# Stick-breaking scores with a second pass over half the partitions, and the memory attention's scaling on GpSimd

## The chip, the core and the metric

The kernel runs on one core of a Trainium2 chip. The metric is device microseconds of that core for one execution of the whole program; lower is better. A core has a matrix engine (TensorE, PE in the rows; its weight loads are listed apart as PEld), a vector engine (VectorE, DVE), a scalar engine (ScalarE, ACT), GpSimd (POOL) and SyncE (SP), which issues most DMAs. Each works through its own queue in order; semaphores join them.

## The reference, cut to what matters

The model is a trunk of two layers over 512 positions and 1024 features. Layer 0 mixes with a gated delta net, layer 1 with stick-breaking attention; in both layers a quarter of the width goes through attention to 256 memory positions. The two pieces that the change touches:

```
z = einsum('bthd,bshd->bhts', q, k) * scale            # stick-breaking: 12 heads of 64 features
log_beta, log_1m_beta = log_sigmoid(z), log_sigmoid(-z) where s < t
tail = reverse cumsum(log_1m_beta) - log_1m_beta
a = exp(log_beta + tail) where s < t
o = einsum('bhts,bshd->bthd', a, v)

s = einsum('bshd,bmhd->bhsm', q, k) * scale             # memory attention: 4 heads of 64 features
p = softmax(s, axis=-1)
o = einsum('bhsm,bmhd->bshd', p, v)
```

## The kernel before

Products of fp32 matrices are made of three passes in a 32-bit format of TensorE that keeps fewer bits: every operand is split into a high part (hi) and the rest (lo), and hi·hi, hi·lo and lo·hi are summed. ScalarE makes the hi parts, VectorE subtracts them for the lo parts (`split_lo`, line 176, always `out = in - hi`).

The order in which instructions stand on each engine is set by a scheduler at build time from the order of the Python generators: `weave` mixes the delta net's recurrence with projections, and in layer 1 `stick_breaking` yields after every unit so that projections and memory attention are put between its units. No order is written out by hand around the change; what it does to the order is shown below.

**Stick-breaking (layer 1).** `sb_qk` projects q and k of one head as one piece: rows 0 to 63 of the result are q, rows 64 to 127 are k. From it three 128x512 tiles are made. `kk` holds k's lo part in rows 0 to 63 and k's hi part in rows 64 to 127. `qh` holds q's hi part in both halves. `ql` holds q's lo part in both halves, which takes two VectorE instructions of 64x512 (line 1075). There are 12 such pieces. `sb_scores` works on units: a unit is some of the four 128-key blocks of one head, and for each block it runs three matmuls into one PSUM bank: `kk` by `qh` over 128 rows (line 1092: lo·hi and hi·hi at once), the mask as a small bf16 matmul of 128 columns (line 1093), and `kk` by `ql` over 128 rows (line 1095: lo·lo and hi·lo). The last pass is the "second pass" of the title; there are 48. ScalarE then computes the logarithms (lines 1100 to 1102), VectorE the softplus `sb_e` (line 1103) and its parts `sp_h` and `sp_l` (lines 1107 and 176), TensorE the running sums (line 1122), ScalarE the exponential `sb_a` (line 1125), VectorE its hi part `sb_ah` (line 1128), GpSimd its lo part `sb_al` (line 1129), and TensorE the product with v (line 1141). A unit's scores, weights and values are issued two units apart.

**Memory attention (both layers).** `mem_attention` has eight units of one head and 256 queries. `scores` runs four matmuls (line 691), takes the maximum (line 694), the exponential with its sums (line 698) and the reciprocal of the sums (line 700, `sm`), and scales the 128x256 halves of `p` by it (line 702, two instructions a unit, 32 in all). `turn` transposes `p` on TensorE (line 711) and splits it into hi and lo; `values` multiplies by v (line 722). One unit's `turn` is issued behind the next unit's `scores`. Layer 0's units run beside the last group of the delta net (288 to 326 us in the profile), layer 1's beside the later stick-breaking units.

GpSimd's queue holds in both places also DMAs: the sums of weights for the MLP (line 882) and a gain (line 973), which waits until the last memory scores have read the buffer it writes.

Of the kernel before, what the change touches and what calls it, by code (L numbers as in the profile page):

```python
# [13 lines left out]
ALU = mybir.AluOpType  # L14
# [28 lines left out]
def f(ap):  # L43
    return ap.bitcast(F32)
# [23 lines left out]
class Trunk:  # L68
# [600 lines left out]
    def mem_attention(self, i, q, alloc, mixT):  # L669

        nc, v = self.nc, self.nc.vector
        kT, vv = self.mk[i], self.mv[i]
        if i == 1:
            wk, wv = alloc("w"), alloc("w")
            for w, d in ((wk, kT), (wv, vv)):
                nc.gpsimd.dma_start(out=w, in_=d[0])
            wk, wv = wk.rearrange("p (c m) -> p c m", c=2), wv.rearrange("p (t h d) -> p t h d", t=2, h=4)
            kT = [self.act.tile([P, 4, NMEM], F32R, name=f"mk0{x}") for x in "hl"]
            vv = self.act.tile([P, 2, 4, 2, 64], F32R, name="mv0")
            for c in range(2):  # L680
                self.both(kT, wk[:, c], c)
            nc.scalar.activation(out=vv[:, :, :, 0], in_=wv, func=AF.Copy)
            self.split_lo(vv[:, :, :, 1], wv, vv[:, :, :, 0])
        pT = {}

        def scores(h, t2):
            b = self.bank("acc").rearrange("p (t m) -> p t m", t=2)
            for j in range(2):
                ts = slice((t2 + j) * P, (t2 + j + 1) * P)
                for n in range(2):  # L690
                    nc.tensor.matmul(b[:, j], lhsT=q[h // 2][h % 2][:, ts], rhs=kT[n][:, h], start=n == 0,
                                     stop=n == 1)
            nm = self.small.tile([P, 2], F32, name="nmx")
            v.tensor_reduce(out=nm, in_=b, axis=AX.X, op=ALU.max, negate=True)
            sm = self.small.tile([P, 2], F32, name="sm")
            p = alloc("p")
            for j in range(2):
                nc.scalar.activation(out=p[:, j], in_=b[:, j], func=AF.Exp, bias=nm[:, j:j + 1],
                                     accum_out=sm[:, j:j + 1])
            v.reciprocal(out=sm, in_=sm)  # L700
            for j in range(2):
                v.tensor_scalar(out=p[:, j], in0=p[:, j], scalar1=sm[:, j:j + 1], scalar2=None, op0=ALU.mult)
            return p

        def turn(h, t2, p):
            if t2 == 0:
                pT[h] = alloc("pTh"), alloc("pTl")
            b = self.bank("acc").rearrange("p (m t) -> p m t", m=2)
            for m in range(2):
                for j in range(2):  # L710
                    nc.tensor.transpose(b[:, m, j * P:(j + 1) * P], p[:, j, m * P:(m + 1) * P], self.ident)
            sl = slice(t2 * P, (t2 + 2) * P)
            for m in range(2):
                nc.scalar.activation(out=pT[h][0][m][:, sl], in_=b[:, m], func=AF.Copy)
                self.split_lo(pT[h][1][m][:, sl], b[:, m], pT[h][0][m][:, sl])

        def values(h):
            p0 = 64 * (h % 2)
            pr, other = slice(p0, p0 + 64), slice(64 - p0, 128 - p0)
            b = self.bank("acc")  # L720
            for n, (k, r) in enumerate(((0, 0), (1, 0), (0, 1), (1, 1))):
                nc.tensor.matmul(b, lhsT=vv[:, k, h].rearrange("p a d -> p (a d)"), rhs=pT[h][r][k], start=n == 0,
                                 stop=n == 3)
            o = alloc("o")
            nc.scalar.activation(out=o[pr], in_=b[other], func=AF.Copy)
            v.tensor_tensor(out=mixT[pr, H + h // 2], in0=b[pr], in1=o[pr], op=ALU.add)

        units = [(h, t2) for h in range(4) for t2 in (0, 2)]
        prev = None
        for u in units + [None]:  # L730
            if u is not None:
                p = scores(*u)
                yield 4 * MM / 2
            if prev is not None:
                turn(*prev)
                yield 4 * MM / 2
                if prev[1] == 0 and prev[0] > 0:
                    values(prev[0] - 1)
                    yield 4 * MM
            prev = (*u, p) if u is not None else None  # L740
        values(3)
        yield 4 * MM
# [319 lines left out]
    def sb_qk(self, pair, hi, lo, pool, out):  # L1062

        nc, v = self.nc, self.nc.vector
        top, low = slice(0, 64), slice(64, P)
        for hh in range(2):
            qh, ql, kk = (pool.tile([P, S], F32R, name=f"sb{n}", bufs=4) for n in ("qh", "ql", "kk"))
            out[hh] = (qh, ql, kk)

            def done(b):  # L1070
                nc.scalar.activation(out=qh[top], in_=b[top], func=AF.Copy, scale=0.125)
                nc.scalar.activation(out=kk[low], in_=b[low], func=AF.Copy)
                nc.scalar.activation(out=qh[low], in_=b[top], func=AF.Copy, scale=0.125)
                for o in (top, low):
                    v.scalar_tensor_tensor(out=ql[o], in0=b[top], scalar=0.125, in1=f(qh[top]), op0=ALU.mult,
                                           op1=ALU.subtract)
                self.split_lo(kk[top], b[low], kk[low])
            yield from self.fm_slices(self.a["w_b_qk"][2 * pair + hh], hi, lo, done)

    def sb_scores(self, u, pool):  # L1080

        nc, v = self.nc, self.nc.vector
        qh, ql, kk = u["qk"][u["pr"].start // 64]
        u["zb"] = zb = self.bank("g")
        n = 0
        u["at"] = {}
        for i in u["blocks"]:
            t0 = i * P
            ks = slice(t0, t0 + P)
            u["at"][i] = slice(n, n + S - t0)  # L1090
            z = zb[:, u["at"][i]]
            nc.tensor.matmul(z, lhsT=kk[:, ks], rhs=qh[:, t0:], start=n == 0, stop=False, skip_group_check=True)
            nc.tensor.matmul(zb[:, n:n + P], lhsT=self.diag_bf, rhs=self.nmask, start=False, stop=False,
                             skip_group_check=True)
            nc.tensor.matmul(z, lhsT=kk[:, ks], rhs=ql[:, t0:], start=False, stop=True, skip_group_check=True)
            n += S - t0
        u["n"] = n
        z = zb[:, :n]
        e = pool.tile([P, S], F32, name="sb_e", bufs=4)[:, :n]
        nc.scalar.activation(out=e, in_=z, func=AF.Abs)  # L1100
        nc.scalar.activation(out=e, in_=e, func=AF.Exp, scale=-1.0)
        nc.scalar.activation(out=e, in_=e, func=AF.Ln, bias=1.0)
        v.scalar_tensor_tensor(out=e, in0=z, scalar=0.0, in1=e, op0=ALU.max, op1=ALU.add)  # L1103
        last = u["blocks"][-1]
        sh = pool.tile([P, n], F32R, name=f"sp_h{last}", bufs=2 if last else 1)
        sl = pool.tile([P, n], F32R, name=f"sp_l{last}", bufs=2 if last else 1)
        v.tensor_copy(out=sh, in_=e)
        self.split_lo(sl, e, sh)
        for i in u["blocks"]:
            u["head"]["sp"][i] = (sh[:, u["at"][i]], sl[:, u["at"][i]])  # L1110
# [258 lines left out]
```

## Time and profile before

| what | value |
| --- | --- |
| median of 3 runs | 1318.02 us (1313.18 to 1321.62) |
| the profiled execution | 1318.39 us |
| its span in the trace | 1316.7 us |
| mean granted TensorE clock | 0.993 of full speed |
| TensorE matmul busy | 1275.9 us (97%) |
| VectorE busy | 861.8 us (65%) |
| ScalarE busy | 717.5 us (54%) |
| GpSimd busy | 163.9 us (12%) |

The busy time of TensorE is modelled from its instructions and overlaps their tails, so 97% does not mean that the array streams all the time; where it streams without a gap, the starts of 512-column matmuls lie 0.23 us apart. The stick-breaking stage runs from about 760 to 926 us.

### The profile page before, as it was taken

Reading aid. Unit: us, or ns where it says so; the run is one execution under the profiler, and the core shown is the slowest. Engines: PE = TensorE matmul, PEld = TensorE weight load, DVE = VectorE, ACT = ScalarE, POOL = GpSimd, SP = SyncE. Lnnn points to the kernel's source line nnn. Section 1 sums busy time; section 2 is a strip of 40 time slices with the busy share of each in tenths; the row PEclk is TensorE's granted clock in tenths of the full one; section 3 lists DMA queues with packets and bytes.
Section 4 is the critical chain, followed back from the end, with each engine's and each line's share of the span. In section 5 each row is a group of like instructions: output and inputs, shape, how many; then the busy total and the mean of one; then the engine's idle time right before and its main releaser. Section 6 shows DMA issues by size and latency. Waiting matters only on the chain.

```text
span 1316.7 us, 18097 instructions
## 1 busy us (share of the span) xinstructions
PE 1275.9 (97%) x6620; PEld 1070.0 (81%) x6620; DVE 861.8 (65%) x1588; ACT 717.5 (54%) x1378; POOL 163.9 (12%) x196
## 2 busy tenths in 40 slices
PE   7999999998999999999999999998999999999997
PEld 7788878887788888878888988786788888878886
DVE  7677695877663264555788678999573255455776
ACT  8654435446455454444565567878455344454561
POOL 2511313010021000000000013223130000000000
PEclk9999999999999999999999999999999999999999
DMA  7551654415689878644454426222679944544441
GB/s 242 192 166 58 161 130 117 123 51 143 210 245 266 233 190 243 195 145 143 148 186 139 157 75 150 76 64 64 208 255 256 257 127 144 148 141 150 152 144 64
DMA packets 82153, 209.39 MB, mean 159 GB/s; under 512 B 6720, under 2 KB 11840, under 8 KB 81616
## 3 DMA queue, kind: packets, MB, share of 16 engines
q1 hardware_dynamic: 62192, 164.12, 37.7%
q0 software_dynamic: 19296, 43.06, 16.4%
q8 instruction: 52, 0.85, 0.3%
q10 hardware_dynamic: 576, 1.05, 0.2%
q14 instruction: 37, 0.30, 0.1%
HBM read 199.29 MB, written 67.63 MB: 203 GB/s over the span
## 4 chain that ended last, share of the span: by engine, by line
PE 80%; DVE 10%; ACT 6%; issue 2%; DMA 1%; POOL 0%; SPq 0%; DVEq 0%; POOLq 0%; ACTq 0%
PE ps_acc L212 45%; PE ps_g L955 21%; PE ps_g L212 4%; PE ps_g L526 1%; PE ps_g L1122 1%; DVE wlo L176 1%; PE ps_g L389 1%; PE ps_g L518 1%; ACT whi L199 1%; PE ps_g L488 1%; ACT scrap L281 1%; DVE cv L360 1%; PE ps_g L295 1%; DVE sb_e L1103 1%; PE ps_acc L1141 1%
## 5 line engine op out<-in xcount | busy, mean ns | idle before, releaser
L212 PE MATMUL ps_acc<-h_hi,whi 128*128 128x512 f32 (+1 forms) x888 | 338.1, 381 | 0.0
L212 PE MATMUL ps_acc<-h_hi,wlo 128*128 128x512 f32 (+1 forms) x888 | 337.5, 380 | 0.0
L212 PE MATMUL ps_acc<-h_lo,whi 128*128 128x512 f32 (+1 forms) x888 | 335.1, 377 | 0.0
L176 DVE TENSOR_TENSOR wlo<-raw,whi 128x1024 fp32r<-128x1024 f32 x134 | 169.2, 1264 | 141.3 <-ACT whi L199 133.9
L955 PE MATMUL ps_g<-whi,sh 128*128 128x512 f32 x784 | 261.1, 395 | 0.0
L199 ACT ACTIVATE whi<-raw 128x1024 fp32r<-128x1024 f32 x134 | 141.8, 1059 | 203.0 <-PE ps_g L955 94.1
L176 DVE TENSOR_TENSOR wlo<-xc,whi 128x1024 fp32r<-128x1024 f32 x89 | 108.8, 1224 | 151.2 <-ACT whi L199 149.0
L212 PEld LDWEIGHTS ps_acc<-h_hi,wlo 128*128 128x128 f32 x888 | 167.5, 189 | 34.0 <-DVE wlo L176 3.9
L212 PEld LDWEIGHTS ps_acc<-h_hi,whi 128*128 128x128 f32 x888 | 167.8, 189 | 28.8 <-ACT whi L199 1.6
L212 PEld LDWEIGHTS ps_acc<-h_lo,whi 128*128 128x128 f32 x888 | 167.9, 189 | 28.4
L955 PEld LDWEIGHTS ps_g<-whi,sh 128*128 128x128 f32 x784 | 147.6, 188 | 34.5
L199 ACT ACTIVATE whi<-xc 128x1024 fp32r<-128x1024 f32 x89 | 94.3, 1060 | 137.1 <-PE ps_g L955 92.5
L955 PE MATMUL ps_g<-wlo,sh 128*128 128x512 f32 x392 | 154.8, 395 | 0.0
L955 PEld LDWEIGHTS ps_g<-wlo,sh 128*128 128x128 f32 x392 | 73.9, 189 | 17.2
L882 POOL DMA_DIRECT2D sum<-w_down x56 | 51.5, 1332 | 181.8 <-DMA sum<-w_down 104.4
L176 DVE TENSOR_TENSOR sh<-ua,sh 128x512 fp32r<-128x512 f32 x98 | 66.7, 685 | 4.7 <-ACT sh L936 4.7
L1129 POOL TENSOR_TENSOR sb_al<-sb_a,sb_ah 128x384 fp32r<-128x384 f32 (+1 forms) x36 | 41.2, 1144 | 154.8 <-DVE sb_ah L1128 133.1
L936 ACT ACTIVATE sh<-ua 128x512 fp32r<-128x512 f32 x98 | 59.9, 618 | 0.3
L212 PE MATMUL ps_acc<-ua 128*128 128x512 f32 x224 | 57.3, 391 | 0.0
L978 POOL DMA_DIRECT2D ua<-park x4 | 2.3, 574 | 388.6 <-DVE sh L176 381.2
L212 PEld LDWEIGHTS ps_acc<-ua 128*128 128x128 f32 x224 | 42.0, 188 | 8.9
L212 PE MATMUL ps_acc<-whi,h_hi 128*128 128x256 f32 (+1 forms) x144 | 44.5, 326 | 0.0
(352 smaller groups left out, 2148.2 us busy)
## 6 DMA issues: line engine op xcount, KB each, us to landing
sum<-w_down POOLq DMA_DIRECT2D x56, 512.0 KB, 9.9
xc<-w_up SPq DMA_DIRECT2D x38, 512.0 KB, 3.9
xc<-w_down SPq DMA_DIRECT2D x30, 512.0 KB, 3.9
xc<-sum SPq DMA_DIRECT2D x29, 512.0 KB, 4.0
sum<-w_down SPq DMA_DIRECT2D x28, 512.0 KB, 6.5
sum<-sum SPq DMA_DIRECT2D x28, 512.0 KB, 5.4
raw<-w_in_a SPq DMA_DIRECT2D x27, 512.0 KB, 3.8
raw<-sum SPq DMA_DIRECT2D x27, 512.0 KB, 3.7
```

Of the source, the lines that this page charges most:

```text
L176: self.nc.vector.tensor_tensor(out=lo, in0=src, in1=f(hi), op=ALU.subtract)
L199: self.nc.scalar.activation(out=hi, in_=raw, func=AF.Copy)
L212: self.nc.tensor.matmul(out, lhsT=l, rhs=r, start=start and k == 0 and i == 0, stop=stop and k == n - 1 and i == 2)
L281: nc.scalar.activation(out=self.scrap(m), in_=x[:, j * m:(j + 1) * m], func=AF.Square, accum_out=ssq[:, j:j + 1])
L295: op = nc.tensor.transpose(b[:, j, i * P:(i + 1) * P], xs[i][:, (kc + j) * P:(kc + j + 1) * P], self.ident)
L360: nc.vector.scalar_tensor_tensor(out=acc[:, j:], in0=b[:, :S - j], scalar=w[:, 3 - j:4 - j], in1=acc[:, j:], op0=ALU.mult, op1=ALU.add)
L389: self.nc.tensor.transpose(tp[:, t], src(t), self.ident)
L488: nc.tensor.matmul(sb[:, j], lhsT=self.sel[:, s4 + j], rhs=ud, start=True, stop=True)
L882: self.tc.keep_in_program_order(nc.gpsimd.dma_start(out=dst, in_=src, accum_op=ALU.add))
L936: nc.scalar.activation(out=s[:, 0], in_=src, func=AF.Copy)
L955: nc.tensor.matmul(y[t], lhsT=l, rhs=r, start=new and d == 0 and z == 0 and m == 0, stop=d == nd - 1 and z == 1 and m == 2, skip_group_che ...
L1129: nc.gpsimd.tensor_tensor(out=u["al"], in0=a, in1=f(u["ah"]), op=ALU.subtract)
```

## The change

The `ql` tile is written in its lower half only (rows 64 to 127), and the second pass reads only those rows of `kk` and `ql`: it multiplies k's hi part with q's lo part and leaves the product of the two lo parts out. It streams as many columns as before, over 64 rows in place of 128. The scaling of `p` moves from VectorE to GpSimd.

```diff
@@ mem_attention, scores
             for j in range(2):
-                v.tensor_scalar(out=p[:, j], in0=p[:, j], scalar1=sm[:, j:j + 1], scalar2=None, op0=ALU.mult)
+                nc.gpsimd.tensor_scalar(out=p[:, j], in0=p[:, j], scalar1=sm[:, j:j + 1], scalar2=None, op0=ALU.mult)
@@ sb_qk, done
-                for o in (top, low):
-                    v.scalar_tensor_tensor(out=ql[o], in0=b[top], scalar=0.125, in1=f(qh[top]), op0=ALU.mult,
-                                           op1=ALU.subtract)
+                v.scalar_tensor_tensor(out=ql[low], in0=b[top], scalar=0.125, in1=f(qh[top]), op0=ALU.mult,
+                                       op1=ALU.subtract)
@@ sb_scores
-            nc.tensor.matmul(z, lhsT=kk[:, ks], rhs=ql[:, t0:], start=False, stop=True, skip_group_check=True)
+            nc.tensor.matmul(z, lhsT=kk[64:, ks], rhs=ql[64:, t0:], start=False, stop=True, skip_group_check=True)
```

Behind line 1075 every line number is one lower in the changed kernel.

How the order moves, first on GpSimd in layer 0's memory attention (`p` is the attention's probabilities, `Q` a tile of the delta net, `sum` the weight sums, `mk0h` the buffer of the gain):

```order
 L510 MEMSET Q 128x4x64 x2
+L702 TENSOR_SCALAR p<-p,sm 128x256 x10
 L882 DMA sum_0_4_603<-w_down 256x512
+L702 TENSOR_SCALAR p<-p,sm 128x256 x2
+L973 DMA mk0h<-norm_post_mlp 128x1024
+L702 TENSOR_SCALAR p<-p,sm 128x256 x4
 L882 DMA sum_1_4_607<-w_down 256x512
 L882 DMA sum_2_4_611<-w_down 256x512
 L882 DMA sum_3_4_615<-w_down 256x512
-L973 DMA mk0h<-norm_post_mlp 128x1024
 L586 TENSOR_TENSOR vb<-vb,fo 128x512
```

The sixteen scalings stand ahead of three of the four sums; the gain's DMA now stands ahead of the last four scalings, the seventh and eighth units'.

On GpSimd near the end of stick-breaking, the rows of before:

```order
L882 DMA sum_1_4_4719<-w_down 256x512
L1129 TENSOR_TENSOR sb_al<-sb_a,sb_ah 128x512
L1129 TENSOR_TENSOR sb_al<-sb_a,sb_ah 128x384 x2
L1129 TENSOR_TENSOR sb_al<-sb_a,sb_ah 128x512
L1129 TENSOR_TENSOR sb_al<-sb_a,sb_ah 128x384
L973 DMA mk0h<-norm_post_mlp 128x1024
```

and of the change:

```order
L882 DMA sum_1_4_4719<-w_down 256x512
L1128 TENSOR_TENSOR sb_al<-sb_a,sb_ah 128x512
L702 TENSOR_SCALAR p<-p,sm 128x256 x2
L1128 TENSOR_TENSOR sb_al<-sb_a,sb_ah 128x384
L702 TENSOR_SCALAR p<-p,sm 128x256 x2
L1128 TENSOR_TENSOR sb_al<-sb_a,sb_ah 128x384
L1128 TENSOR_TENSOR sb_al<-sb_a,sb_ah 128x512
L702 TENSOR_SCALAR p<-p,sm 128x256 x2
L973 DMA mk0h<-norm_post_mlp 128x1024
```

A pair of scalings now stands between the `sb_al` subtractions, one pair for one or two of them.

On VectorE, where the projections of stick-breaking's first pieces are taken apart:

```order
 L176 TENSOR_TENSOR wlo<-raw,whi 128x1024
-L1075 SCALAR_TENSOR_TENSOR sbql<-ps_acc,sbqh 64x512 x2
+L1074 SCALAR_TENSOR_TENSOR sbql<-ps_acc,sbqh 64x512
 L176 TENSOR_TENSOR sbkk<-ps_acc,sbkk 64x512
 L176 TENSOR_TENSOR wlo<-raw,whi 128x1024
-L1075 SCALAR_TENSOR_TENSOR sbql<-ps_acc,sbqh 64x512 x2
+L1074 SCALAR_TENSOR_TENSOR sbql<-ps_acc,sbqh 64x512
 L176 TENSOR_TENSOR sbkk<-ps_acc,sbkk 64x512
```

One instruction a piece is gone and its neighbours keep their places. In TensorE's queue the three matmuls of a block keep their places, too, except in the last units.

## Rows read from the trace of the kernel before

**Rows 1.** The page, part 1: busy time, share, instructions.

```profile
PE 1275.9 (97%) x6620; PEld 1070.0 (81%) x6620; DVE 861.8 (65%) x1588; ACT 717.5 (54%) x1378; POOL 163.9 (12%) x196
```

**Rows 2.** Windows of stick-breaking, early and late: busy us, PEclk, DMA share, GB/s.

```profile
755.00:835.00 80.00, 79.90 (x432) 67.23 (x431) 64.39 (x102) 57.10 (x104) 18.43 (x18) 1.00 0.47 122
835.00:926.00 91.00, 82.50 (x462) 66.50 (x461) 85.82 (x163) 72.59 (x160) 28.81 (x27) 1.00 0.22 57
```

**Rows 3.** The chain of waits by line, 755 to 835, then 835 to 926 us.

```profile
by line: PE ps_acc L212 63.3%; PE ps_g L1122 14.8%; PE ps_acc L1141 7.2%; PE ps_g L1095 5.7%; PE ps_g L1092 4.5%; PE ps_g L1093 2.1%; PE ps_acc L691 1.2%; DVE sp_h L1107 1.0%; DVE sb_e L1103 0.8%; DVE sb_ah L1128 0.4%; issue 0.0%
...
by line: issue 9.6%; DVE sb_e L1103 7.6%; DVE sp_l L176 7.5%; DVE sp_h L1107 7.5%; DVE p L702 4.5%; ACT sb_e L1101 3.8%; ACT p L698 3.7%; ACT whi L199 3.7%; POOL sb_al L1129 3.7%; ACT sb_e L1100 3.6%; PE ps_g L1122 3.6%; DVE sb_ah L1128 3.3
```

**Rows 4.** PE's timeline in one unit's scores: start, duration, line, tiles, shape.

```profile
783.18 0.22 PE L1092 MATMUL ps_g<-sbqh,sbkk 128*128 128x128 f32 x1
783.25 0.23 PE L1093 MATMUL ps_g<-nmask,diag_bf 128*128 128x128 bf16 x1
783.28 0.30 PE L1095 MATMUL ps_g<-sbql,sbkk 128*128 128x128 f32 x1
783.43 0.33 PE L1092 MATMUL ps_g<-sbqh,sbkk 128*128 128x256 f32 x1
```

**Rows 5.** Second passes: their weight loads, ns min/median/max; then groups early and late.

```profile
L1095 PEld LDWEIGHTS ps_g<-sbql,sbkk x48: 190/200/203, 762.7 to 910.2; 128*128 128x128 f32 x48
...
L1095 PE MATMUL ps_g<-sbql,sbkk 128*128 128x128 f32 (+3 forms) x23 | 8.9, 387 | 0.0
...
L1095 PE MATMUL ps_g<-sbql,sbkk 128*128 128x512 f32 (+3 forms) x25 | 9.8, 393 | 0.0
```

**Rows 6.** DVE groups, 835 to 926 us: busy us, mean ns, idle before.

```profile
L176 DVE TENSOR_TENSOR sp_l<-sb_e,sp_h 128x384 fp32r<-128x384 f32 x13 | 10.3, 795 | 0.2
...
L702 DVE TENSOR_SCALAR p<-p,sm 128x256 f32<-128x256 f32 x14 | 6.9, 532 | 0.1
L1075 DVE SCALAR_TENSOR_TENSOR sbql<-ps_acc,sbqh 64x512 fp32r<-64x512 f32 x10 | 6.8, 680 | 0.2
...
L1107 DVE CAST sp_h<-sb_e 128x384 fp32r<-128x384 f32 x13 | 6.0, 465 | 0.1
...
L1107 DVE CAST sp_h<-sb_e 128x512 fp32r<-128x512 f32 x8 | 4.7, 587 | 0.1
```

**Rows 7.** Line 702's durations over the whole run, ns min/median/max.

```profile
L702 DVE TENSOR_SCALAR p<-p,sm x32: 341/349/1409, 293.7 to 919.2; 128x256 f32<-128x256 f32 x32
```

**Rows 8.** DVE's timeline, undisturbed and beside GpSimd.

```profile
840.52 0.36 DVE L1107 CAST sp_h<-sb_e 128x384 fp32r<-128x384 f32 x1
840.91 0.56 DVE L176 TENSOR_TENSOR sp_l<-sb_e,sp_h 128x384 fp32r<-128x384 f32 x1
...
846.41 1.36 DVE L176 TENSOR_TENSOR sp_l<-sb_e,sp_h 128x384 fp32r<-128x384 f32 x1
...
848.88 0.42 DVE L1107 CAST sp_h<-sb_e 128x512 fp32r<-128x512 f32 x1
```

**Rows 9.** POOL's timeline: that subtraction, a later one, a memset, the gain's DMA.

```profile
846.06 1.29 POOL L1129 TENSOR_TENSOR sb_al<-sb_a,sb_ah 128x512 fp32r<-128x512 f32 x1 [5.71 <-DVE sb_ah L1128]
849.13 1.04 POOL L1129 TENSOR_TENSOR sb_al<-sb_a,sb_ah 128x384 fp32r<-128x384 f32 x1 [1.78 <-PE ps_acc L1141]
...
291.77 0.31 POOL L510 MEMSET Q<- 128x256 f32 x1 [8.03 <-PE ps_g L526]
...
310.86 0.61 POOL L973 DMA_DIRECT2D mk0h<-norm_post_mlp  x1 [13.32 <-PE ps_acc L691]
```

**Rows 10.** Waits of PE late in stick-breaking (total us, times, longest).

```profile
PE ps_acc L1141 <- POOL sb_al L1129: 1.7, 3, 0.8
```

**Rows 11.** Layer 0's memory attention: window, DVE group, PE's wait for it.

```profile
288.00:326.00 38.00, 32.58 (x207) 28.90 (x207) 28.02 (x80) 23.50 (x81) 4.80 (x7) 0.91 0.55 139
...
L702 DVE TENSOR_SCALAR p<-p,sm 128x256 f32<-128x256 f32 x16 | 4.9, 348 | 0.0
...
PE ps_acc L711 <- DVE p L702: 2.2, 3, 1.3
```

## The prediction, made before the changed kernel ran

> **What bounds the kernel now.** I read the page's busy shares first: TensorE is busy 97% of the span, VectorE 65%, GpSimd 12% [rows 1]. That is an average over stages, so I asked for the windows of the three places that the change touches. The reader is to see that the stick-breaking stage falls in two. From 755 to 835 us TensorE is busy 79.9 of 80 us, VectorE 64.4. From 835 to 926 us VectorE is busy 85.8 of 91 us, ScalarE 72.6, GpSimd 28.8, and TensorE's modelled 82.5 leaves at least 8.5 us free [rows 2]. The chain of waits says the same: early it is TensorE's lines almost alone, late it runs through VectorE's and ScalarE's short instructions, with line 702 itself at 4.5% of 91 us [rows 3]. So early every nanosecond added on TensorE counts and VectorE's relief is worth nothing; late it is the other way round. The granted clock is 1.00, the 2.4 GHz level, in both. In layer 0's memory attention (288 to 326 us) no engine is full: TensorE 32.6, VectorE 28.0 of 38 us [rows 11].
>
> **The second pass on TensorE.** Nothing is taken off it: 48 matmuls stay, of the same columns, 23 early and 25 late [rows 5]. What is new is that a matmul over rows 64 to 127 stands between two that use all 128 rows. The trace has no such change of rows, so its price p for one second pass must be bounded. Below: zero, since columns and weight loads stay; a gain only if a weight load of half the rows hid better, worth at most what is exposed today. That is read from the starts: `kk` by `qh` over 128 columns lets the next matmul start 0.07 us later, while the second pass over as many columns holds it for 0.15 us (783.28 to 783.43) [rows 4]: 0.08 us of a weight load that the short mask matmul before it cannot hide. Above: nothing of the neighbours overlaps any more. The mask matmul's record lasts 0.23 us where the next starts after 0.03, so 0.20; the second pass's lasts 0.30 where the next starts after 0.15, so 0.15 [rows 4]; a weight load of 0.20 us [rows 5] ahead of each change of rows, 0.40; less the 0.08 exposed already: 0.67 us. I take p = 0.09 us, one more weight load exposed as one is today, since that is the nearest row: also a neighbour that cannot be overlapped in full, and it costs that much. Early that is 23 x 0.09 = **+2.1 us** (bounds 23 x -0.08 = -1.8 and 23 x 0.67 = +15.4). Late 25 x 0.09 = 2.3 us fits into TensorE's 8.5 us.
>
> **VectorE late in stick-breaking.** Two things leave its queue between 835 and 926 us: half of ten line 1075 instructions, 5 x 0.680 = 3.4 us, and 14 scalings, 6.9 us [rows 6]. GpSimd takes them. An operation of this kind by GpSimd is in no row. The nearest below is a memset of 128x256, 0.31 us, which reads nothing; above, the subtraction of 128x384 with two inputs, 1.04 us [rows 9]. I take 0.7 us, the subtraction's time by columns (256 of 384), because a scaling reads and writes as it does. Fourteen are 9.8 us, and GpSimd then has 28.8 + 9.8 = 38.6 of 91 us: not a bound.
>
> But GpSimd's work slows VectorE. While `sb_al` ran from 846.06 to 847.35, `sp_l` of 128x384, begun at 846.41, took 1.36 us in place of 0.56 [rows 8, 9]. Over the window: 13 such `sp_l` at 0.795 against 0.56 are 3.1 us, 13 casts at 0.465 against 0.36 are 1.4, 8 casts at 0.587 against 0.42 are 1.3, 14 scalings at 0.532 against the median 0.349 are 2.6 [rows 6 to 8]: 8.4 us lost beside 28.8 us of GpSimd, 0.29 us per us. The new 9.8 us thus cost VectorE 2.8 us. Net relief: 3.4 + 6.9 - 2.8 = 7.5 us of 85.8. The Trainium skill (SBUF — State Buffer, Who interferes with whom) has a harder rule: a VectorE instruction with two SBUF inputs and a GpSimd instruction that reads SBUF exclude each other, and the loser waits in full. The trace agrees for the single case just read; by the rule's worst case all 9.8 us would come back as stalls, the relief would be 3.4 + 6.9 - 9.8 = 0.5 us, and the total below would be 1320.0. I stay with 0.29, the measured share, since VectorE's reads of PSUM and its other one-input work go on.
>
> How much of 7.5 us reaches the end? All of it if VectorE alone held the stage. But the chain there is shared: of it, line 702 is 4.5% of 91, 4.1 us [rows 3], and ScalarE stands close behind with 72.6 us. I take **-4.5 us** (bounds -7.5 and 0).
>
> The new wait on GpSimd: a pair of scalings waits for the reciprocal and stands ahead of `sb_al` subtractions, which TensorE's line 1141 needs. Today that line waits for them 1.7 us in three places [rows 10]; a unit's values are issued two units behind its weights, which covers a pair of 1.4 us, and I cost it at nothing. If that cover were gone it would be up to 8 x 1.4 us (a rival below).
>
> **Early in stick-breaking**, the other seven of the 12 line 1075 instructions and two scalings go as well; TensorE is the bound there, so they are worth nothing. **Layer 0's memory attention:** VectorE loses 16 scalings, 4.9 us; TensorE waited for them 2.2 us in three places [rows 11]. By GpSimd a pair takes 1.4 us in place of 0.7, but starts at once on an idle engine. The DMA of the gain now stands ahead of the last two units' scalings: its 13.3 us wait for the last scores [rows 9] was harmless, and now holds the seventh unit's scaling until those are done, plus its own 0.61 us, about 1 us once. The sums' DMAs behind them move by less than the 11.2 us of the scalings and are read only in the MLP. I take 0 (bounds: -3, the 2.2 us and part of the rest, to 8 x 0.7 = +5.6).
>
> **The sum.** Against the profiled execution's own 1318.4 us (0.4 us above the median of the runs shown, span 1316.7): 1318.4 + 2.1 - 4.5 + 0 = **1316.0 us**. About 1%, 13 us, is what a measurement of this kernel tells from no change, so this is a forecast of no change.
>
> **The rivals.**
> *The change of rows empties the array.* TensorE waits at both ends of the second pass until the matmul before has left it. The place is the 48 second passes; the price is 0.20 + 0.15 = 0.35 us with the weight loads hidden, 0.67 without. At 0.35: early 23 x 0.35 = 8.1; late 25 x 0.35 = 8.8, which uses up TensorE's 8.5 us and leaves, say, half of the 4.5: 1318.4 + 8.1 - 2.2 = 1324. At 0.67: early 15.4, late 16.8 - 8.5 - 4.5 = +3.8, 1337.6: slower. It decides, over 1%, from 48p - 8.5 - 4.5 = 13.2, p = 0.55 us. For it: nothing of this sort is in the trace, and the tails that could be exposed are long. Against it: the mask's change from 32-bit to bf16 and back passes without a full tail [rows 4]. The Trainium skill (TensorEngine Tiling (Array Packing), Key Properties) says that changing the tiling mode drains the TensorE, a mode of 64 rows being one of its list; by that rule this rival holds, and no run so far shows it. Chance 25%.
> *GpSimd becomes a gate.* Each of eight pairs holds up a subtraction that TensorE needs at once: 11.2 us in place of the relief, 1318.4 + 2.1 + 11.2 - 4.5 = 1327. For it: both waits of line 1141 for `sb_al` exist already. Against it: GpSimd idles 60% of the stage. Chance 8%.
> *The whole relief arrives.* -7.5 late, -3 in layer 0, second passes free: 1318.4 - 10.5 = 1308. For it: VectorE is the fullest engine; against: ScalarE's share of the chain. Chance 11%.
> That the change does not do what it says can be left out: the order shows the scalings on GpSimd and one instruction fewer a piece.
>
> **How the numbers follow.** The forecast has 56%, with 1310 to 1322 of its own. The range must reach over the lower half of the emptied array and the gate, and down to the whole relief: 1308 to 1332; left out are the emptied array's dearer half (12%) and half of the whole relief (5%). Slower by over 1%: that dearer half and a little of the gate, 13%. Faster by over 1% (under 1305): 4%. Within 1%: 83%.
>
> **What would show it.** The window from 755 to 835 us, at the same work, is the test of p: about 2 us longer is my sum, 8 or more the emptied array; a second pass's start gap over 128 columns would go from 0.15 to about 0.24 or to 0.5. VectorE's groups late should lose lines 702 and half of 1075, and `sp_l` and the casts grow slower by some 2 to 3 us in all. The GpSimd scaling should last 0.5 to 0.9 us. I am wrong if the early window shrinks, if line 711 or 1141 becomes the longest wait of TensorE, or if the late window does not shorten at all.

## The result: 1.2% slower, and the profile after

The changed kernel takes 1335.6 us (median of 6) against 1320.7 us of the kernel before (median of 6): ratio 1.0118, 95% interval 1.0099 to 1.0136. The prediction was 1316.0 us with a range of 1308 to 1332; it was wrong. One run of a later version took 2120.33 us at a mean granted clock of 0.577, where the others of that version lie at 0.994 or above; it is left out of that version's numbers. The profiled execution of the changed kernel took 1337.6 us, its span 1335.9, 19.2 us more than the span of before. The page, part 1, of the changed kernel, beside [rows 1]:

```profile
PE 1296.1 (97%) x6620; PEld 1081.0 (81%) x6620; DVE 847.3 (63%) x1544; ACT 718.8 (54%) x1378; POOL 196.1 (15%) x228
```

VectorE did lose 14.5 us of work and GpSimd took 32.2 us on. TensorE, with as many instructions, is busy 20.2 us longer. To see where, I took the same work in both profiles, by the starts of equal instructions. The windows of the changed kernel that hold the work of [rows 2]:

```profile
764.00:851.00 87.00, 87.00 (x433) 69.82 (x432) 60.61 (x95) 57.92 (x107) 20.89 (x20) 1.00 0.42 112
851.00:945.20 94.20, 89.42 (x464) 70.46 (x462) 79.07 (x141) 72.75 (x158) 42.56 (x39) 0.98 0.21 57
```

Early 87.0 us in place of 80, late 94.2 in place of 91. So 7.0 + 3.2 us of the 19.2 lie in stick-breaking, and 9.0 stand already ahead of it.

**Early: the second pass.** One unit's scores on TensorE's timeline, the one of [rows 4], in the changed kernel:

```profile
794.40 0.22 PE L1091 MATMUL ps_g<-sbqh,sbkk 128*128 128x128 f32 x1
794.47 0.23 PE L1092 MATMUL ps_g<-nmask,diag_bf 128*128 128x128 bf16 x1
794.63 0.32 PE L1094 MATMUL ps_g<-sbql,sbkk 64*128 64x128 f32 x1
794.88 0.38 PE L1091 MATMUL ps_g<-sbqh,sbkk 128*128 128x256 f32 x1
795.11 0.23 PE L1092 MATMUL ps_g<-nmask,diag_bf 128*128 128x128 bf16 x1
```

and the row of before that follows those of [rows 4]:

```profile
783.60 0.23 PE L1093 MATMUL ps_g<-nmask,diag_bf 128*128 128x128 bf16 x1
```

Read the starts. The second pass starts 0.16 us behind the mask matmul, where it was 0.03. It holds the next matmul for 0.25 us, where it was 0.15; and that one, of 256 columns, holds its own follower for 0.23, where the same matmul of before, started at 783.43, held it for 0.17 (to 783.60). Together 0.13 + 0.10 + 0.06 = 0.29 us for one second pass. The pass itself is no longer (0.32 against 0.30), its weight load is shorter, 183 ns against 200 in [rows 5]. What is lost is the overlap with both neighbours. Over the 23 early passes it adds up; the first unit's first matmul and the start of the 23rd second pass, before:

```profile
762.60 0.22 PE L1092 MATMUL ps_g<-sbqh,sbkk 128*128 128x128 f32 x1
...
833.32 0.42 PE L1095 MATMUL ps_g<-sbql,sbkk 128*128 128x384 f32 x1
```

and in the changed kernel:

```profile
771.58 0.22 PE L1091 MATMUL ps_g<-sbqh,sbkk 128*128 128x128 f32 x1
...
849.36 0.43 PE L1094 MATMUL ps_g<-sbql,sbkk 64*128 64x384 f32 x1
```

70.72 us before, 77.78 now: 7.06 us for 22 passes and the entry of one more (0.13), so 0.315 us a pass.

**Layer 0's memory attention.** Line 702 over the whole run and one pair of it on POOL's timeline, and what TensorE waited for it from 285 to 345 us (total, times, longest):

```profile
L702 POOL TENSOR_SCALAR p<-p,sm x32: 912/928/1594, 292.9 to 937.8; 128x256 f32<-128x256 f32 x32
...
299.74 1.83 POOL L702 TENSOR_SCALAR p<-p,sm 128x256 f32<-128x256 f32 x2 [2.71 <-DVE sm L700]
```

```profile
PE ps_acc L711 <- POOL p L702: 5.3, 8, 1.5
```

A scaling takes 0.93 us on GpSimd, 0.35 on VectorE [rows 7]; a pair 1.83. The waits of line 711 rise from 2.2 us in three places [rows 11] to 5.3 in eight. And then there is the clock. Three windows of the stage, the number ahead of the last two being the granted clock; the kernel before:

```profile
289.00:298.00 9.00, 8.00 (x43) 7.97 (x44) 5.85 (x16) 4.63 (x14) 4.20 (x6) 0.62 0.32 65
298.00:307.00 9.00, 7.22 (x56) 6.55 (x56) 8.44 (x25) 6.30 (x24) 0.00 (x0) 1.00 1.10 228
307.00:319.00 12.00, 10.18 (x68) 8.69 (x66) 9.18 (x28) 8.67 (x30) 0.61 (x1) 1.00 0.26 67
```

and the changed kernel:

```profile
289.00:298.00 9.00, 5.02 (x34) 4.30 (x35) 5.97 (x14) 4.58 (x13) 4.77 (x6) 0.91 0.12 47
298.00:307.00 9.00, 9.00 (x42) 8.53 (x42) 3.70 (x10) 4.54 (x16) 3.65 (x4) 0.52 0.00 0
307.00:319.00 12.00, 10.13 (x47) 8.87 (x47) 5.73 (x16) 5.36 (x20) 4.57 (x6) 0.63 0.47 87
```

In the changed kernel TensorE works only 5.0 of the first 9 us, and behind that its clock is granted at about half, the 1.2 GHz level, for most of the next 21 us: it is then busy all the time and does 42 matmuls' records where 56 went through. Weighting each window with one minus its clock gives 9 x 0.09 + 9 x 0.48 + 12 x 0.37 = 9.6 us of lost clock; in the profile of before 9 x 0.38 = 3.4. By this estimate some 6 of the 9 us are clock and the rest the waits themselves; profiles of equal code, read below, put it at some 5. Note that the kernel before has such a stretch too, behind a wait of 1.8 us:

```profile
290.00 3.36 PE L526 MATMUL ps_g<-X,Q 128*128 128x64 f32 x16 [1.82 <-DVE Q L519]
```

**Late.** VectorE's busy time falls from 85.8 [rows 2] to 79.1 us in these windows. They are cut by TensorE's work, and the second lacks three of VectorE's instructions: it holds 141, where 163 less 14 scalings and 5 subtractions is 144. Over the same instructions the relief is 5.3 us:

```profile
849.05:945.05 96.00, 91.37 (x476) 71.97 (x474) 80.37 (x144) 73.83 (x161) 42.41 (x39) 0.98 0.21 55
```

The stage gets 3.2 us longer all the same: TensorE's busy time rises from 82.5 to 89.4 of it. And line 1140 (line 1141 of before) now waits once for 1.4 us for `sb_al`, ahead of which GpSimd works through a pair of scalings and the gain's DMA:

```profile
PE ps_acc L1140 <- POOL sb_al L1128: 2.1, 2, 1.4
...
926.22 2.92 POOL L702 TENSOR_SCALAR p<-p,sm 128x256 f32<-128x256 f32 x2 [1.39 <-PE ps_acc L711]
929.09 0.64 POOL L973 DMA_DIRECT2D mk0h<-norm_post_mlp  x1
929.75 1.01 POOL L1128 TENSOR_TENSOR sb_al<-sb_a,sb_ah 128x384 fp32r<-128x384 f32 x1
```

TensorE's clock is low behind that wait, too (0.57 on average from 931 to 935 us). What this one wait costs by itself no run shows.

### The profile page after: what moved, and what is told of

It reads as the page before. It is cut to its first block, busy times and chain, and to the rows that moved or that the text cites. A ratio compares the mean times of both kernels' runs of the same rounds, so it can differ in the third digit from the quotient of the medians.

```text
span 1335.9 us, 18096 instructions
## 1 busy us (share of the span) xinstructions
PE 1296.1 (97%) x6620; PEld 1081.0 (81%) x6620; DVE 847.3 (63%) x1544; ACT 718.8 (54%) x1378; POOL 196.1 (15%) x228
## 4 chain that ended last, share of the span: by engine, by line
PE 84%; DVE 7%; ACT 4%; issue 2%; POOL 1%; DMA 1%; DVEq 0%; POOLq 0%; ACTq 0%
PE ps_acc L212 46%; PE ps_g L955 21%; PE ps_g L212 4%; PE ps_g L1121 2%; PE ps_g L526 1%; PE ps_g L518 1%; DVE wlo L176 1%; PE ps_g L1094 1%; POOL p L702 1%; PE ps_acc L1140 1%; PE ps_g L389 1%; ACT whi L199 1%; PE ps_g L488 1%; DVE cv L360 1%; ACT scrap L281 1%
```

## The experiments

My theory after the two traces had three independent parts: about 0.32 us of TensorE's time for each change from 128 rows to 64 and back; a longer pair of scalings in layer 0 that TensorE waits for, with the clock falling behind the waits; and late a relief of VectorE that the stage does not need. The rivals: that the changed order of instructions did it, that each 64-row matmul is dear by itself, that GpSimd's queue (the gain's DMA) holds things up. Each experiment's ratio compares it with 13 to 29 runs of the kernel before made beside it (medians 1319.4 to 1320.3 us); the interval behind it is the one of 95%.

### The parts alone

**The rows alone** (line 702 stays on VectorE):

```
-                for o in (top, low):
-                    v.scalar_tensor_tensor(out=ql[o], ...
+                v.scalar_tensor_tensor(out=ql[low], ...
...
-            nc.tensor.matmul(z, lhsT=kk[:, ks], rhs=ql[:, t0:], ...
+            nc.tensor.matmul(z, lhsT=kk[64:, ks], rhs=ql[64:, t0:], ...
```

> The change of rows alone: the second score pass over rows 64 to 127 and one subtraction a piece; the scalings of the memory attention stay on VectorE in both layers. Theory A (a 64-row matmul between two 128-row matmuls costs TensorE about 0.32 us, as the linear drift of 7.0 us over 23 early second passes says): layer 0's memory attention as before, so the first second pass starts at 762.7 us as before (within 0.5); the window from 755 to 835 us holds 7 us more work time; late the 25 passes cost at most what they did with the scaling, so 1.005 to 1.008 of the kernel before, +7 to +10 us. Rival B (the early drift comes from the scaling's new order on the engines and not from the rows): within 2 us of the kernel before, the early drift gone.

Measured: 1328.0 us (median of 4), ratio 1.0076 (1.0048 to 1.0104). The early drift is there in full, 77.82 us where it was 70.72:

```profile
760.29 0.22 PE L1091 MATMUL ps_g<-sbqh,sbkk 128*128 128x128 f32 x1
...
838.11 0.43 PE L1094 MATMUL ps_g<-sbql,sbkk 64*128 64x384 f32 x1
```

Behind it only 0.6 us more are lost to the end: late, TensorE's slack and the subtractions saved absorb the 25 other passes. One point missed: the first second pass starts 2.2 us earlier than before, not at the same time. Nothing in the code ahead of it differs; in this execution TensorE's clock stayed at 1.00 from 289 to 346 us, where the profile of before has 0.62 over the first 9 us:

```profile
289.00:298.00 9.00, 7.59 (x62) 7.04 (x63) 8.15 (x26) 6.82 (x23) 4.19 (x6) 1.00 0.53 86
```

That pointed to the clock as the cause of the scatter between runs.

**The scaling on GpSimd in layer 0 alone:**

```
-                v.tensor_scalar(out=p[:, j], ...
+                (nc.gpsimd, v)[i].tensor_scalar(out=p[:, j], ...
```

> The scaling on GpSimd in layer 0's memory attention alone; rows and layer 1 as in the kernel before. Theory A (16 scalings at 0.93 us, two in a row before TensorE's line 711 can turn a unit's weights, TensorE waits and its granted clock falls): the first second pass starts about 9 us later than in the kernel before, and nothing more is lost or won behind it, +8 to +10 us. Rival B (the shift of 9 us needs both edits, or it is given back in the MLP's DMA-bound stretches): +0 to +3 us.

Measured: 1323.5 us (median of 7), 1.0039 (1.0023 to 1.0055), so 3 to 7 us: between the ranges of the two theories. In its profile the first second pass starts 6.4 us late, and nothing is given back behind it: the theory's mechanism holds, its size was read from one pair of profiles and was too high by some 4 us. TensorE's wait and the second window, as above for the changed kernel:

```profile
PE ps_acc L711 <- POOL p L702: 5.7, 8, 1.5
```

```profile
298.00:307.00 9.00, 9.00 (x46) 8.53 (x45) 4.09 (x11) 4.57 (x17) 3.64 (x4) 0.56 0.00 0
```

**The scaling on GpSimd in layer 1 alone** (`(v, nc.gpsimd)[i]`):

> The scaling on GpSimd in layer 1's memory attention alone; rows and layer 0 as before. Theory A (late in stick-breaking VectorE loses 14 scalings of 0.35 to 0.53 us but waits for a 1.9 us pair on GpSimd and for its port come instead): between -4 and +3 us, taken 0; the first second pass at 762.7 us as before, the second passes 23 to 48 within 3 us of the kernel before. Rival B (GpSimd is a gate: pairs of 1.9 us ahead of the sb_al subtractions that line 1141 needs): +5 us or more, with line 1141's waits for GpSimd risen from 1.7 us to 8 or more.

Measured: 1321.7 us (median of 10), 1.0021 (1.0006 to 1.0036): 1 to 5 us slower, at the upper end of the theory's range. One point missed: the first second pass starts at 765.4 us, 2.7 later than before, though this edit touches nothing ahead of it; 1.2 us of that go with the clock in layer 0's memory attention (0.86 in place of 0.91 from 284 to 321 us, read below). The gate is not there: line 1141 waits 1.4 us in all for `sb_al`, 1.7 before [rows 10]. The window that holds the work of 835 to 926 us, VectorE's `sp_l` over 128x384 and 128x512, and TensorE's new wait:

```profile
837.40:929.90 92.50, 83.60 (x463) 67.55 (x461) 82.62 (x148) 72.39 (x160) 43.64 (x40) 0.98 0.22 59
```

```profile
L176 DVE TENSOR_TENSOR sp_l<-sb_e,sp_h 128x384 fp32r<-128x384 f32 x13 | 11.1, 855 | 0.1
L176 DVE TENSOR_TENSOR sp_l<-sb_e,sp_h 128x512 fp32r<-128x512 f32 x8 | 9.2, 1155 | 0.2
```

```profile
PE ps_acc L711 <- POOL p L702: 2.9, 4, 1.6
```

VectorE gave 6.9 us of scalings away [rows 6], and over the same instructions (the window holds one cast too few) its busy time fell by 2.5 only: its other instructions got 4.2 us longer beside 14.8 us of new GpSimd work, 0.28 us per us, near the 0.29 of the prediction. Most of it are the `sp_l` of 128x512, 774 ns before. The rule cited there from the Trainium skill (SBUF — State Buffer, Who interferes with whom), taken at its worst, would by estimate have brought back all 14.8 us, more than VectorE gave away; the trace shows 4.2. What remained bought nothing, and TensorE now waits 2.9 us for pairs in four places. The three parts add up to 0.76 + 0.39 + 0.21 = 1.36%, within the uncertainty of the whole change's 1.18%.

**One subtraction a piece without the change of rows:** the second pass keeps 128 rows, the upper 64 rows of queries being zeros in four fixed tiles that GpSimd writes once.

```
+            ql = self.qls[(2 * pair + hh) % 4]
...
+        for q in k.qls:
+            nc.gpsimd.memset(f(q[:64]), 0.0)
```

> The second pass stays over all 128 rows, but its upper 64 rows of queries are zeros, written once into four fixed tiles by GpSimd at the start; so VectorE still does one subtraction a piece in place of two. The scalings stay on VectorE. Theory A (the loss of the change is the change of rows, the one subtraction less is a relief where VectorE is the fullest engine): early no drift at all, late 0 to 3.4 us won, so -3 to 0 us. Rival B (the drift comes from the moved subtraction, whose absence lets other VectorE work come in front of what TensorE waits for): +5 us or more with the same linear drift as in the changed kernel.

Measured: 1317.9 us (median of 10), 0.9997 (0.9984 to 1.0011). No early drift: the second passes 1 to 23 keep their distances to 0.01 us. So the drift belongs to the rows. What VectorE's relief of 3.4 us is worth late is too small for these times, but the profiles show it. The stage's first matmul in this run:

```profile
764.33 0.22 PE L1092 MATMUL ps_g<-sbqh,sbkk 128*128 128x128 f32 x1
```

From its start to the end of the span, at 1316.6, it is 552.3 us, in place of 554.1 before (762.60 to 1316.7). In the four runs of this document that leave all of this as it was (the scaling on GpSimd or split in layer 0 alone, the two fillings of the kernel before) it is 553.9 to 554.0. So about half of the relief, 1.8 us, arrives.

### What a change of rows costs

**Second passes of a unit side by side**, so that a unit with two blocks changes rows once:

```
         for i in u["blocks"]:
...
-            nc.tensor.matmul(z, lhsT=kk[64:, ks], ...
...
+        for i in u["blocks"]:
+            nc.tensor.matmul(zb[:, u["at"][i]], lhsT=kk[64:, i * P:(i + 1) * P], rhs=ql[64:, i * P:], ...
```

> As the run of the rows alone, but a unit's second passes stand one behind the other at the unit's end, so that a unit with two blocks changes from 128 rows to 64 and back once and not twice. 12 of the 36 units have two blocks. Theory A (the price of 0.32 us is one of the change of rows, in and out): the grouped passes of a unit start one behind the other at their columns' pace (about 0.06 us apart for 128 columns), the early drift over 23 passes falls from 7.0 to about 5 us, the time to about 2 to 4 us under that of the rows alone, 1.004 to 1.006 of the kernel before. Rival B (each matmul over 64 rows is dearer by itself): the drift stays at 7 us, the time at that of the rows alone within 1 us.

Measured: 1324.1 us (median of 8), 1.0039 (1.0022 to 1.0057), half the loss of the rows alone, though the two intervals overlap a little. The first unit of this run (two of its second passes in one row) and its 23rd second pass:

```profile
763.46 0.22 PE L1091 MATMUL ps_g<-sbqh,sbkk 128*128 128x128 f32 x1
763.52 0.23 PE L1092 MATMUL ps_g<-nmask,diag_bf 128*128 128x128 bf16 x1
763.56 0.36 PE L1091 MATMUL ps_g<-sbqh,sbkk 128*128 128x256 f32 x1
763.76 0.23 PE L1092 MATMUL ps_g<-nmask,diag_bf 128*128 128x128 bf16 x1
763.92 0.49 PE L1096 MATMUL ps_g<-sbql,sbkk 64*128 64x128 f32 x2
...
839.59 0.43 PE L1096 MATMUL ps_g<-sbql,sbkk 64*128 64x384 f32 x1
```

76.13 us, 5.4 more than before. Among these 23 passes six pairs stand side by side, so there are 17 changes in place of 23: 16 x 0.315 + 0.13 = 5.2. Per pass it would have been 7.1. The price is one of the change, not of the matmul. One point missed: the two grouped passes start 0.17 us apart (763.92 and 764.09 in the trace; the row shows them as one), not 0.06. The Trainium skill (TensorEngine Tiling (Array Packing), Key Properties) says that a change of tiling mode drains the TensorE; these rows agree, 0.32 us in and out.

### What layer 0 lost

**The pair split between two engines in layer 0:**

```
+                (v if i or j == 0 else nc.gpsimd).tensor_scalar(out=p[:, j], ...
```

> Layer 0's memory attention: of each pair of scalings the first stays on VectorE, the second goes to GpSimd, so that the two run side by side (0.93 us in place of 1.86 on GpSimd or 0.70 on VectorE); layer 1 and the rows as before. Theory A (the loss in layer 0 is the pair's length ahead of TensorE's line 711 and the fall of its clock that the waits bring): the waits of line 711 for line 702 fall from 5.7 us to about 3, and the time to +0 to +2 us over the kernel before. Rival B (the loss comes from GpSimd's queue, the gain's DMA standing ahead of scalings): the time stays at +4 to +6 us, with the longest wait of line 711 that behind the DMA of line 973.

Measured: 1320.0 us (median of 10), 1.0005 (0.9992 to 1.0019). TensorE's wait is back at its old size:

```profile
PE ps_acc L711 <- DVE p L702: 2.3, 3, 1.0
```

The gain's DMA stands ahead of the last units' scalings here too, so the queue was not the cause; the length of the pair was.

**Filling TensorE's wait, first try.** The 1.8 us wait for `Q` at 288 us, behind which the clock of the kernel before falls, is filled with eight matmuls whose results nobody reads, in the free half of `Q`'s bank:

```
+                if gi == 2 and L == 32:
+                    for t in range(4):
+                        nc.tensor.matmul(qa[:, t % 4, P // 2:], lhsT=u["UI"][:, t % 4, 0], rhs=u["XT"][:, t % 4], ...
```

> The kernel before with eight more matmuls of 128x64 (about 1 us, results unused) in the last group of layer 0's delta-rule stage, where TensorE waited 1.8 us for Q (288 to 290 us) just before its clock fell to 0.50. Theory A (TensorE's clock falls there because TensorE stood idle, and what the fall costs is a large part of layer 0's memory attention): the granted clock stays at 1.00 from 290 to 300 us and the stage ends 2 to 4 us earlier than in the profile of before, the time 0 to 3 us under the kernel before. Rival B (the clock falls there for another reason, or the fall costs nothing): the same low stretch, and the time of the kernel before or 1 us more.

Measured: 1321.7 us (median of 10), 1.0024 (1.0008 to 1.0039). It tested nothing of the kind, because the filling waited as well (line 524 is the filling):

```profile
PE ps_g L524 <- DVE Q L520: 1.7, 1, 1.7
```

**Second try, twelve in a bank of their own**, ahead of which no reading stands:

```
+            if gi == 2 and L == 32:
+                qf = self.bank4()
+                for t in range(12):
+                    nc.tensor.matmul(qf[:, t % 4, :P // 2], lhsT=u["UI"][:, t % 4, 0], rhs=u["XT"][:, t % 4], ...
```

> The kernel before with twelve more matmuls of 128x64 (about 1.4 us, results unused) in a bank of their own, at the same place as in the run before this one: there they stood behind Q's reading of their bank and waited with it, so TensorE stood idle all the same (1.7 us). Now they can run while Q is made. Theory A (the clock falls to 0.50 after 290 us because TensorE stood idle, and the fall is what makes layer 0's memory attention dearer): the wait of line 526 for Q falls from 1.8 us to under 0.6, the granted clock stays at 1.00 up to 298 us, and the time is 1 to 3 us under the kernel before. Rival B (another idle stretch behind it sets the clock): the clock falls all the same, a few us later, and the time is within 1 us of the kernel before or above it.

Measured: 1316.8 us (median of 12), 0.9985 (0.9974 to 0.9996). TensorE's timeline (line 524 is the filling, each matmul of which leaves two records; line 531 is what was line 526) and the first window:

```profile
287.00 2.84 PE L524 MATMUL ps_g<-XT,UI 128*128 128x64 f32 x24
289.68 1.95 PE L531 MATMUL ps_g<-X,Q 128*128 128x64 f32 x16
```

```profile
289.00:298.00 9.00, 8.43 (x71) 7.81 (x71) 7.51 (x24) 5.99 (x22) 4.18 (x6) 1.00 0.43 67
```

No wait is left ahead of the product with `Q`, and the clock stays at 1.00. The stretch of layer 0's memory attention, from the first matmul of line 691 to the last one of line 722, takes 30.8 us (from 284.12 to 314.89) in place of 32.9 (285.14 to 318.04), though TensorE does more work.

One profile doesn't settle it, since the clock stayed up in that of the rows alone as well. But six profiles have the code of the kernel before up to the end of this stretch. In them it takes 30.1 us where the clock is 1.00 from 284 to 321 us (rows alone), 32.9 twice at 0.91 (before, side by side), and 34.1 to 34.2 three times at 0.86 (layer 1 alone, zeros, the pair split in layer 1). The code is equal and the time goes with the clock: the weighting above would give 3.4 us at 0.91, and 2.8 were lost. Three profiles have the filling in a bank of its own and no whole pair on GpSimd in layer 0, this one and the last two of this document: none has a clock under 1.00 in this stretch. Of the eight in which TensorE waits 1.7 or 1.8 us there, again without whole pairs on GpSimd in layer 0, seven have. The one without a fall shows that the wait doesn't always bring it, and that the filling costs 0.7 us (30.8 against 30.1) where it isn't needed. The scatter agrees, though a run's mean clock also counts low stretches elsewhere (at 55 and 335 us in the profile of before): of 29 runs of the kernel before beside these, the six with a mean clock of 0.991 took 1320.2 to 1322.0 us, the five at 0.997 and 0.998 took 1314.6 to 1317.1; of the 12 filled ones eleven lie at 0.995 to 0.998 and 1315.5 to 1317.8 us. That the clock's fall costs time here is shown, and that it comes far more often where TensorE stands idle ahead of it.

**The same filling in the changed kernel:**

> The changed kernel with the twelve filling matmuls in layer 0's delta-rule stage. Theory A (in the changed kernel the waits of line 711 for GpSimd, 1.5, 0.5 and 0.6 us from 292 us on, let the clock fall even where TensorE was busy up to then): a stretch at 0.50 all the same, a little later, and the time within 2 us of the changed kernel, 1.010 to 1.012 of the kernel before. Rival B (the fall is set by the 1.8 us wait for Q alone): the clock stays at 1.00 through the memory attention, and 3 to 6 us of the layer's loss are gone, 1.007 to 1.009.

Measured: 1335.3 us (median of 4), 1.012 (1.0100 to 1.0141), as without it. Its first two windows:

```profile
289.00:298.00 9.00, 6.65 (x52) 5.81 (x52) 5.66 (x14) 4.44 (x13) 4.76 (x6) 0.93 0.09 37
298.00:307.00 9.00, 9.00 (x41) 8.53 (x40) 3.34 (x10) 4.21 (x14) 3.64 (x4) 0.50 0.00 0
```

The wait for `Q` is gone, those for GpSimd's `p` (5.6 us) follow, and the clock falls behind them instead. So in the changed kernel the waits for the scalings are enough for a fall, without the one for `Q`.

### Is there a better version?

**The pair split in layer 1** (`v if i == 0 or j == 0 else nc.gpsimd`):

> Layer 1's memory attention: the first scaling of a pair stays on VectorE, the second goes to GpSimd; layer 0 and the rows as before. Theory A (the late stage loses by the pair of about 2 us that TensorE's line 711 waits for, and by the stalls of VectorE beside GpSimd's work, which take back most of its relief): line 711's waits for line 702 fall from 2.9 us (whole pair on GpSimd) to under 1, VectorE's sp_l lose about half of the 3.9 us that they gained, and the time comes to -1 to +1 us of the kernel before. Rival B (any work of this kind on GpSimd late costs the stage): +2 us or more, as with the whole pair.

Measured: 1319.4 us (median of 10), 0.9998 (0.9983 to 1.0012). Line 711 waits 1.0 us for GpSimd, and `sp_l` is as fast as before:

```profile
L176 DVE TENSOR_TENSOR sp_l<-sb_e,sp_h 128x384 fp32r<-128x384 f32 x13 | 10.3, 792 | 0.2
L176 DVE TENSOR_TENSOR sp_l<-sb_e,sp_h 128x512 fp32r<-128x512 f32 x8 | 6.2, 774 | 0.2
```

Half the GpSimd work brings not half of the stalls on these but none; they seem to depend on what happens to run side by side, which no run tests. VectorE's busy time falls by 2.2 us over the same instructions, with no gain in time: from the stage's first matmul to the end it is 554.4 us, 0.3 more than before (whole pairs: 555.2).

**Zeros and filling together:**

> Two edits together: the second pass over 128 rows with zeros in the upper rows of queries (one subtraction a piece less on VectorE), and the twelve filling matmuls in a bank of their own. Theory A: -1 to -4 us of the kernel before. Rival B (neither buys anything): within 1 us.

Measured: 1314.8 us (median of 11), 0.9974 (0.9959 to 0.9988): faster than both kernels, by about a quarter of a per cent against the kernel before. Its interval overlaps that of the filling alone, so the times don't tell what the zeros add. Its profile does:

```profile
760.02 0.22 PE L1097 MATMUL ps_g<-sbqh,sbkk 128*128 128x128 f32 x1
```

With a span of 1312.3 us it is again 552.3 us from there to the end, where the filling alone has 553.9: the zeros add 1.6 us.

**And with all pairs split as well:**

> The version with zeros and filling matmuls, and of each pair of scalings in both layers the second on GpSimd. Theory A (split pairs cost TensorE nothing, and VectorE's relief late is not what the stage waits for): within 2 us of that version, so 2 to 5 us under the kernel before. Rival B (with the pairs split the relief comes through): 6 us or more under the kernel before.

Measured: 1318.0 us (median of 10), 0.9983 (0.9970 to 0.9996). VectorE has more relief, and the time is not shorter: in the profile it is 554.0 us from the stage's first matmul to the end, so there the split pairs take back what the zeros gave.

## Why the prediction was wrong

**The second pass, +2.1 early: wrong in size.** Measured 7.1 us; 0.315 us a pass in place of 0.09. The step that failed is the choice between the bounds. I took the nearest row, a weight load that a short neighbour cannot hide, as the model for a change of rows. That row has the neighbours overlapping in part; with the change of rows the second pass starts 0.13 us later behind the mask matmul, and the next matmul 0.10 later behind it. The tails that the prediction added up for its rival (0.20 + 0.15 = 0.35 us, at 25%) were the right model. Late, the rival's sum, 8.8 us of extra passes meeting 8.5 us of slack, was near: the rows alone lost 0.6 us there where the zeros won 1.8, so the 25 passes cost some 2.4.

**Layer 0, 0: wrong in size, over the upper bound in the whole change.** The text says that a pair takes 1.4 us in place of 0.7 "but starts at once on an idle engine". The time of a scaling by GpSimd, taken as 0.7 us from the subtraction by columns, was too small, 0.93 measured. And an idle engine that takes 1.83 us for a pair is still 1.1 us later for TensorE than one that takes 0.70; TensorE had too little other work to cover that, and its waits rose by 3.1 us. Measured: 3 to 7 us by the part alone, about the bound of +5.6; 8.6 in the profile of the whole (41.5 us in place of 32.9 from the first matmul of line 691 to the last one of line 722). The bound counted waits at full clock only. The fall of the clock behind a wait had no term, though 0.91 stood in the row that I used [rows 11].

**Late, -4.5: wrong in sign.** Of the relief forecast on VectorE, 7.5 us, 5.3 came. The step that failed is not the share that reaches the end, as the prediction took it from the chain (4.5 of 7.5): of the 3.4 us of subtractions 1.8 arrive where they go alone. It is the new wait on GpSimd, which was costed at nothing. With whole pairs line 711 waits 2.9 us for them in the run of layer 1 alone, and the stage to the end gets 1.1 us longer instead of shorter; with split pairs, 0.3; together with the zeros split pairs leave nothing of the 1.8 us. That the waits are what takes the scalings' relief away is read from these rows; no run keeps the relief and takes the waits away. In the whole change the longest of these waits is one for `sb_al` (1.4 us), as the prediction's second rival has it, but once and not eight times. The parts alone make 0.6 + 1.1 = 1.7 of the 3.2 us; why the rest comes only with both is open.

**The range.** Each rival was weighed by itself. Two of them came together, an emptied array (1324) and waits for GpSimd, these above all at line 711 in layer 0, where I put none, and less at `sb_al` late, where I put them. Neither excludes the other, and the range had no case with both. (Of line 1141 the prediction says that both waits for `sb_al` exist already; [rows 10] has three.)

## What to carry to other kernels

A matmul over 64 rows between matmuls over 128 saved nothing here and cost its neighbours' overlap. If half the rows are idle, filling them with zeros once avoided the whole price; putting the 64-row matmuls side by side avoided part of it. Moving an instruction to an idle, slower engine is costed by its latency towards the next reader first and by the busy time that it frees last: late, the same stage won 1.8 us by 3.4 us of instructions that were dropped, and nothing by 6.9 us that were moved. And where a stage is full of short waits, look at the granted clock in small windows: a wait of a microsecond or two on TensorE can be followed by several at half speed, and a few idle matmuls may be cheaper than that (0.7 us against 2.8 here).

## What the runs showed of the hardware

- A change from 128 rows to 64 and back costs TensorE about 0.32 us in and out, with one 64-row matmul between or with two; the same matmul over 128 rows, half of them zeros, costs nothing more than before.
- Scaling 128x256 by a column takes 0.93 us on GpSimd (median), 0.35 on VectorE.
- GpSimd's one-input scalings can slow VectorE's two-input subtractions: `sp_l` of 128x512 rose from 0.77 to 1.16 us with pairs on GpSimd in layer 1, and not at all with single ones.
- TensorE's granted clock fell to 0.50 behind waits of 1.5 to 1.8 us, in some executions and not in others. With equal code, one stretch of layer 0 took 30.1, 32.9 or 34.2 us with mean clocks of 1.00, 0.91 or 0.86; this goes a good way to account for the 1314 to 1322 us over which the kernel before scatters.
